# Weight splits held behind activation splits at two stage changes, the last FFN's gate and up projection turned round, and the last output columns cut 384 and 128

## The chip, the cores and the metric

One core of a Trainium2 chip runs the whole kernel. The metric is the time of one execution on the device in microseconds: the median of 3 runs of the kernel before is 1436.4 us (1436.33 to 1437.58). Engines by the profile's names: PE (TensorE, matrix products), PEld (its weight loads), DVE (VectorE), ACT (ScalarE), POOL (GpSimd), SP (SyncE, which issues nearly all DMAs).

## What is computed

Two transformer blocks over 256 tokens of width 1024, in float32:

```python
x = x + 0.5 * swiglu(rmsnorm(x), ...)           # FFN 1 (width 2816)
x = x + hybrid_mixer(rmsnorm(x), ...)           # mixer 1
x = x + 0.5 * swiglu(rmsnorm(x), ...)           # FFN 2
x = rmsnorm(x, final_norm)
h = ffn_sublayer(x + pos, ...); hc = ffn_sublayer(ctx, ...)   # FFN 3, 256 + 256 tokens
h = h + mods[5] * mixer(h, hc)                  # mixer 2
h = h + 0.5 * gate * ((silu(hn @ Wg) * (hn @ Wu)) @ Wd)       # FFN 4 ("the last FFN"), 256 tokens
return rmsnorm_2(h, g_final)
```

Shifts, scales and gates of the second block come from a small product with `w_ada`, which runs as a filler beside the other work.

## The kernel before

Every product is made of three: a float32 operand is split into a high and a low part (high by an ACT copy, low by a DVE subtraction), and high x high, high x low and low x high are accumulated (`mm3`, line 129, and `mm3r`, line 134, for several outputs in turn). A weight unit is 128 x 1024: `load` (line 96) fetches it by SP into one of 4 `raw` buffers, and `split` (line 107) writes `wh` (ACT) and `wl` (DVE), usually into one of 5 buffers each of the pool `wsp`, or into two of 18 slots (`salloc`, line 53). Activations are transposed on PE (line 147), and `split_out` (line 150) writes them as `XH` and `XL` (ACT, then DVE).

The order on each engine is fixed when the program is built. A scheduler goes by the order in which the code is written, but it issues ahead of its turn what it expects to be ready sooner. `tc.issue_after(ins)` keeps what is traced in its block behind `ins` on the same engine: an order of issue and no wait for `ins` to finish. Line 1110 uses it for one early unit.

**FFN 1, 2 and 4** (`ffn2tok`, line 316) take two token tiles of 128 tokens (t = 2 and 3). The up half runs over 11 chunks of 512 columns (256 of gate, 256 of up). In a chunk (`proj_chunk`, line 246) the activations are the stationary operand and the weights move, 512 columns at a time: 2 token tiles x 8 slices of K x 3 = 48 matmuls. `sink_gu` (line 331) makes silu(gate) * up with tokens on the partitions, and because the down half needs that transposed, `later` (line 343) adds 4 transposes to each chunk (line 348) and one `split_out`; they are issued in the next chunk (`flush_at=2`), those of the last chunk in the down half. In the down half each f of 22 brings one unit and 12 matmuls on 4 PSUM outputs of 512 (line 385). The last 4 f come output by output. With `fine` (last FFN) the last output of the last tile is made in two halves of 256 columns (line 396), so that the final norm can begin on the first. PSUM has 4 buffers of the tag `acc` and 4 of `tr`.

**FFN 3** (`ffn4tok`, line 413) has 512 tokens and does it the other way: weights stationary, tokens moving (`projT2`, line 303), so that the product comes out transposed. Its first 4 units (f = 0 and 1), split early into slots by `ahead` (line 1185), are used in halves of 256 tokens, which gives the second half of the tokens time to arrive.

**A change of stage** goes: last product, residual, norm (DVE, ACT, a power on POOL, DVE), 4 transposes for each half of a tile, XH, XL, first product of the next stage. `norm_end` (line 216) puts the transposes behind a number of matmuls of 512 columns that are traced after it: `late`, one number for each half (lines 1181, 1216, 1230). `self.last` (line 165) holds the two instructions of the newest `split_out` of a transposed half.

**Mixer 2** (`mixer2`, line 793) ends with the output projection `w_o` in two chunks (line 1064), the second tile by tile (`last_by_tile`), so that all its 4 units are split before its first tile is done. The last FFN's first chunk goes tile by tile too (`first_by_tile`).

The last function `after` (line 1238) makes the final norm of a tile and stores it in two DMAs of 512 columns (lines 1250 and 1252), one from ACT's queue and one from SP's.

## Time and profile before

| | us |
|---|---|
| median of 3 runs | 1436.4 |
| profiled execution, its own time | 1433.65 |
| span of the profiled execution, first to last instruction | 1431.8 |
| PE busy | 1408.0 |
| DVE busy | 920.8 |
| ACT busy | 627.2 |
| POOL busy | 32.6 |

The profile is of one execution. A row of the timeline gives the start in us from the span's beginning, the duration (of the merged group where a count follows), the engine, the line, the operation and what it writes and reads, how many were merged, and in brackets how long the engine stood idle before it and whose end let it go on. Matmuls are pipelined: one that shows 0.40 us can be followed 0.23 us later by the next, so the pace is read from the starts. Names of buffers in a row are not in the order of operands: `acc<-wh,XH` is a product of the two, whichever moves.

### The profile page before, as it was taken

What the parts mean: (1) busy time and instruction counts of PE and PEld (TensorE: products, weight loads), DVE (VectorE), ACT (ScalarE), POOL (GpSimd) and SP (SyncE); (2) the same over time, 40 slices, a digit from 0 to 9 for tenths busy, and PEclk for the clock granted to TensorE, in tenths of its full rate; (3) what the DMA queues carried; (4) which work ended last, traced back from release to release, by engine and by line L of the source; (5) the groups of instructions that cost most, each with busy time, mean ns of one, the idle gap of its engine ahead of it and who ended that gap; (6) DMA issues with size and microseconds to landing.
All of it is one profiled execution on the core that took longest, in us unless ns stands there. A gap on an engine that the chain in (4) does not pass through costs nothing. (4 is left out here: it accounts for less than half of the span.)

```text
span 1431.8 us, 17904 instructions
## 1 busy us (share of the span) xinstructions
PE 1408.0 (98%) x6782; PEld 1148.9 (80%) x6782; DVE 920.8 (64%) x1296; ACT 627.2 (44%) x904; POOL 32.6 (2%) x49
## 2 busy tenths in 40 slices
PE   7999999999999999999999999999999999999997
PEld 5877887778888888888888887889888888788886
DVE  6988456878988474543555447376886566755545
ACT  5445347465446442322122224353855454544442
POOL 0000000000000000000000001001010000000000
PEclk9999999999999999999999999999999999999999
DMA  8888645457887663643665443324236665555661
GB/s 285 297 267 271 213 135 196 133 178 251 301 276 244 211 213 105 193 146 102 191 205 176 152 142 103 108 101 143 87 120 189 192 192 177 183 182 180 184 183 71
DMA packets 73015, 260.65 MB, mean 182 GB/s; under 512 B 8140, under 2 KB 8672, under 8 KB 72928
## 3 DMA queue, kind: packets, MB, share of 16 engines
q1 hardware_dynamic: 72640, 258.98, 57.0%
q8 instruction: 53, 0.87, 0.2%
q10 hardware_dynamic: 288, 0.52, 0.1%
q14 instruction: 34, 0.28, 0.1%
HBM read 258.32 MB, written 1.14 MB: 181 GB/s over the span
## 5 line engine op out<-in xcount | busy, mean ns | idle before, releaser
L68 DVE TENSOR_TENSOR wl<-raw,wh 128x1024 fp32r<-128x1024 f32 (+1 forms) x385 | 464.3, 1211 | 335.7 <-ACT wh L65 331.6
L65 ACT ACTIVATE wh<-raw 128x1024 fp32r<-128x1024 f32 (+1 forms) x385 | 403.2, 1050 | 604.9 <-PE acc L78 466.5
L78 PE MATMUL acc<-wh,XH 128*128 128x512 f32 (+1 forms) x992 | 337.5, 398 | 0.3 <-ACT t L65 0.3
L78 PE MATMUL acc<-wh,XL 128*128 128x512 f32 (+1 forms) x992 | 333.7, 393 | 0.2 <-DVE XL L68 0.2
L78 PE MATMUL acc<-wl,XH 128*128 128x512 f32 (+1 forms) x992 | 332.0, 393 | 0.3 <-DVE wl L68 0.3
L78 PE MATMUL acc<-wh,S 128*128 128x512 f32 x872 | 237.3, 395 | 0.6 <-DVE t L71 0.6
L78 PEld LDWEIGHTS acc<-wh,XL 128*128 128x128 f32 x992 | 185.2, 188 | 42.6 <-DVE XL L68 1.3
L78 PEld LDWEIGHTS acc<-wl,XH 128*128 128x128 f32 x992 | 184.9, 188 | 42.4 <-DVE wl L68 1.8
L78 PEld LDWEIGHTS acc<-wh,XH 128*128 128x128 f32 x992 | 184.7, 188 | 41.4 <-ACT XH L65 0.5
L78 PEld LDWEIGHTS acc<-wh,S 128*128 128x128 f32 x872 | 162.8, 188 | 39.4 <-DVE t L71 1.4
L518 DVE SCALAR_TENSOR_TENSOR S<-raw,S 128x1024 f32<-128x1024 f32 x112 | 136.6, 1220 | 73.7 <-DMA raw<-in_w_ada 72.9
L78 PE MATMUL acc<-XH,wh 128*128 128x512 f32 (+1 forms) x456 | 137.3, 379 | 0.0
L78 PE MATMUL acc<-XL,wh 128*128 128x512 f32 (+1 forms) x456 | 137.2, 379 | 0.0
L78 PE MATMUL acc<-XH,wl 128*128 128x512 f32 (+1 forms) x456 | 137.2, 379 | 0.0
L78 PE MATMUL acc<-wl,S 128*128 128x512 f32 x436 | 132.6, 393 | 0.0
L78 PEld LDWEIGHTS acc<-XL,wh 128*128 128x128 f32 x456 | 83.9, 188 | 17.5
L78 PEld LDWEIGHTS acc<-XH,wl 128*128 128x128 f32 x456 | 83.9, 188 | 17.5
L78 PEld LDWEIGHTS acc<-XH,wh 128*128 128x128 f32 x456 | 83.7, 188 | 17.5
L78 PEld LDWEIGHTS acc<-wl,S 128*128 128x128 f32 x436 | 81.9, 188 | 18.5
L147 PE MATMUL tr<-ident,t 128*128 128x128 f32 x200 | 32.2, 285 | 11.6 <-DVE t L68 9.3
L65 ACT ACTIVATE XH<-tr 128x512 fp32r<-128x512 f32 x44 | 26.0, 597 | 37.9 <-PE tr L147 37.3
L78 PE MATMUL tr<-S,S 128*128 128x258 f32 (+3 forms) x288 | 42.0, 299 | 0.2 <-ACT S L65 0.2
(161 smaller groups left out, 855.9 us busy)
## 6 DMA issues: line engine op xcount, KB each, us to landing
raw<-in_gu SPq DMA_DIRECT2D x176, 512.0 KB, 4.3
raw<-in_d SPq DMA_DIRECT2D x88, 512.0 KB, 4.3
raw<-in_w_ada SPq DMA_DIRECT2D x72, 512.0 KB, 4.5
raw<-in_w_in SPq DMA_DIRECT2D x68, 512.0 KB, 3.8
raw<-in_w_qk SPq DMA_DIRECT2D x16, 512.0 KB, 3.6
bc<-modd SPq DMA_DIRECT2D x10, 512.0 KB, 4.9
raw<-in_w_out SPq DMA_DIRECT2D x8, 512.0 KB, 3.7
raw<-in_w_b SPq DMA_DIRECT2D x8, 512.0 KB, 4.2
```

Of the source, the lines that this page charges most:

```text
L65: return self.nc.scalar.activation(out=out, in_=in_, func=func, **kw)
L68: return self.nc.vector.tensor_tensor(out=out, in0=a, in1=b, op=op)
L78: self.nc.tensor.matmul(out, l, r, start=start, stop=stop, **kw)
L147: self.nc.tensor.transpose(tr[:, j, :], src[:, j * P:(j + 1) * P], self.ident)
L518: nc.vector.scalar_tensor_tensor(out=junk, in0=raw, scalar=1.0, in1=cb[r], op0=ALU.mult, op1=ALU.mult, accum_out=mc[:, o:o + 1])
```

## The change

Seven edits in one. First, `split` can hold its two instructions behind `self.last` on their engines while a counter `held` is above zero. Second, `ffn4tok` sets `held` to 4 after its first part, so the units of f = 2 and 3 are held. Third, mixer 2 calls `ahead` before the second `w_o` chunk: the last FFN's first 4 units are loaded and split there into 8 slots; after the last FFN's first chunk they are freed and `held` is 3. Fourth, in the last FFN the chunks 1 to 10 become 20 steps of `projT2` with stationary weights and 256 tokens moving, and the weights are packed to suit (`pack_guT`); silu * up then comes out transposed and is split directly. Fifth, at f = 0 of every down half of `ffn2tok` the matmuls of the first two outputs come before those of the other two. Sixth, `late` becomes (24, 27) at mixer 2 and (20, 23) at the last FFN. Seventh, the last output is made in 384 and 128 columns, and the final scaling of the first 128 columns goes from ACT to DVE, with a DMA of its own from SP.

```diff
@@ -35,6 +35,7 @@
         self.pre = []
         self.deferred = []
         self.later_pe = []
+        self.held = 0
 
 
     def nm(self, s):
@@ -110,8 +111,12 @@
         else:
             wh = self.wsp.tile([P, 1024], F32R, tag="wh", name=self.nm("wh"))
             wl = self.wsp.tile([P, 1024], F32R, tag="wl", name=self.nm("wl"))
-        self.act(wh[:, :n], raw[:, :n])
-        self.tt(wl[:, :n], raw[:, :n], wh[:, :n].bitcast(F32), ALU.subtract)
+        if self.held:
+            self.held -= 1
+            with self.tc.issue_after(self.last[0].ins), self.tc.issue_after(self.last[1].ins):
+                self.split_out(wh[:, :n], wl[:, :n], raw[:, :n])
+        else:
+            self.split_out(wh[:, :n], wl[:, :n], raw[:, :n])
         if self.fill_every:
             self.fill_count += 1
             if self.fill_count % self.fill_every == 0 and next(self.filler, 0) is None:
@@ -313,7 +318,7 @@
                 self.mm(ps, wl[:, s], a, False, k == xk - 1)
 
 
-    def ffn2tok(self, Wgu, Wd, xts, rows, sink, after, skew=4, first_by_tile=False, fine=False, mid=None, ahead=None):
+    def ffn2tok(self, Wgu, Wd, xts, rows, sink, after, skew=4, cols=False, first_by_tile=False, w0=(), fine=False, mid=None, ahead=None):
 
 
         hT = {}
@@ -324,7 +329,7 @@
                 hT[g] = (self.salloc([P, 4, 256], F32R), self.salloc([P, 4, 256], F32R))
             return hT[g] + (f % 4,)
 
-        for c in range(11):
+        for c in range(1 if cols else 11):
             self.fill_every = 2 if self.filler is not None and 1 <= c < 10 else 0
             trs = []
 
@@ -353,6 +358,24 @@
                 self.defer(later)
 
             self.proj_chunk(Wgu, 4 * c, xts, sink_gu, flush_at=2, last_by_tile=c == 0 and first_by_tile)
+            if c == 0 and w0:
+                for w in w0:
+                    self.sfree(*w)
+                self.held = 3
+        if cols:
+            toks = slice(xts[0][0] * P, xts[0][0] * P + 256)
+            for f in range(2, NF):
+                self.fill_every = 3 if self.filler is not None and f < 20 else 0
+                ws = [self.unit(Wgu[2 * f + j]) for j in range(2)]
+                pss = [self.psum("acc", [P, 256]) for _ in range(2)]
+                self.projT2(pss, ws, toks)
+                sil, h = self.t2([P, 256]), self.t2([P, 256])
+                self.act(sil, pss[0], AF.Silu)
+                self.tt(h, pss[1], sil, ALU.mult)
+                hh, hl, sl = dest(f)
+                self.split_out(hh[:, sl, :], hl[:, sl, :], h)
+                if f == 2:
+                    self.flush()
         if mid is not None:
             mid()
         ps = {}
@@ -382,7 +405,8 @@
                 self.mm3r(groups[3:], False, True)
                 sink(t, d, ps[t, d])
                 continue
-            self.mm3r(groups, f == 0, False)
+            for q in (groups[:2], groups[2:]) if f == 0 else (groups,):
+                self.mm3r(q, f == 0, False)
             if f == 0:
                 self.flush()
         ws = [self.unit(Wd[f]) for f in range(NF - skew, NF)]
@@ -393,8 +417,8 @@
         for i, (t, _) in enumerate(xts):
             for d in range(2):
                 if fine and i == 1 and d == 1:
-                    for q in (slice(0, 256), slice(256, 512)):
-                        pq = self.psum("tr", [P, 256])
+                    for q in (slice(0, 384), slice(384, 512)):
+                        pq = self.psum("tr", [P, q.stop - q.start])
                         for f in range(NF - skew, NF):
                             (wh, wl), (hh, hl, sl) = ws[f - NF + skew], dest(f)
                             w = slice(512 + q.start, 512 + q.stop)
@@ -441,6 +465,7 @@
                 for w in ws:
                     self.sfree(*w)
                 f = 2
+                self.held = 4
             for f in range(f, f1):
                 self.fill_every = 1 if f0 + 4 < f or f0 else 0
                 ws = [self.unit(Wgu[2 * f + j]) for j in range(2)]
@@ -790,7 +815,7 @@
         self.stt(out, z, 0.0, e, ALU.min, ALU.subtract)
 
 
-    def mixer2(self, xts, x, after):
+    def mixer2(self, xts, x, after, ahead):
         nc, A = self.nc, self.A
         lat = xts[2:]
         W = A["w_in2"]
@@ -1061,6 +1086,8 @@
                 self.tt(x[t][:, s], x[t][:, s], y, ALU.add)
                 after(t, n)
 
+            if n == 1:
+                ahead()
             self.proj_chunk(A["w_o"], 4 * n, [(t, mx[t]) for t, _ in lat], sink_o, last_by_tile=n == 1)
         self.sfree(*H.values(), *MX.values(), *SO.values(), *GA.values())
 
@@ -1213,7 +1240,7 @@
         def after(t):
             if t == 0:
                 prep()
-            xm.append((t, self.norm_xT(x[t], t, *mods[1 if t < 2 else 0], (21, 24))))
+            xm.append((t, self.norm_xT(x[t], t, *mods[1 if t < 2 else 0], (24, 27))))
 
         self.ffn4tok(A["gu3"], A["d3"], xts, res_gate, after, w3)
         self.sfree(x[0], x[1], *mods[0], *mods[1])
@@ -1227,9 +1254,17 @@
                 mods[2] = (self.mod_scale(7, 0, gF), self.mod(6, 0))
             fin[t] = self.norm_half(x[t], fin.get(t), d, mods[2][0])
             if d == 1:
-                xf.append((t, self.norm_end(fin[t], t, mods[2][1], (18, 21))))
-
-        self.mixer2(xm, x, after)
+                xf.append((t, self.norm_end(fin[t], t, mods[2][1], (20, 23))))
+
+        w4 = []
+
+        def ahead():
+            for u in range(4):
+                dst = self.salloc([P, D], F32R), self.salloc([P, D], F32R)
+                w4.append(self.split(*self.load(A["gu4"][u]), dst))
+
+        self.mixer2(xm, x, after, ahead)
+        self.pre = list(w4)
         G[0] = self.mod(8, 0)
         gl = self.bcast(A["g_final"])
 
@@ -1246,12 +1281,15 @@
             if d == 0 or q.stop < 512:
                 return
             r = self.rstd_of(ss, len(part))
-            self.act(ys[0], ys[0], scale=r)
-            nc.scalar.dma_start(out=self.out[t - 2][:, 0:512], in_=ys[0])
+            o = self.out[t - 2]
+            self.act(ys[0][:, 128:], ys[0][:, 128:], scale=r)
+            nc.scalar.dma_start(out=o[:, 128:512], in_=ys[0][:, 128:])
             self.ts(ys[1], ys[1], r)
-            nc.sync.dma_start(out=self.out[t - 2][:, 512:], in_=ys[1])
-
-        self.ffn2tok(A["gu4"], A["d4"], xf, {}, res_gate, after, first_by_tile=True, fine=True)
+            nc.sync.dma_start(out=o[:, 512:], in_=ys[1])
+            self.ts(ys[0][:, :128], ys[0][:, :128], r)
+            nc.sync.dma_start(out=o[:, :128], in_=ys[0][:, :128])
+
+        self.ffn2tok(A["gu4"], A["d4"], xf, {}, res_gate, after, first_by_tile=True, fine=True, w0=w4, cols=True)
 
 
 COLS = [("b_a", 2), ("conv_w", 12), ("gnorm", 1), ("wa2", 256), ("qk_w", 48), ("qk_b", 16),
@@ -1303,6 +1341,12 @@
     return pack_proj(w)
 
 
+def pack_guT(g, u):
+
+    gt, ut = pack_T(g), pack_T(u)
+    return np.concatenate([pack_gu(g, u)[:4], np.stack([gt, ut], axis=1)[2:].reshape(-1, P, D)])
+
+
 def pack_d4(w):
     parts = []
     for f0, f1 in ((0, 12), (12, 22)):
@@ -1341,7 +1385,7 @@
     a["gu1"] = pack_gu(i["ffn1_w_gate"][0], i["ffn1_w_up"][0])
     a["gu2"] = pack_gu(i["ffn2_w_gate"][0], i["ffn2_w_up"][0])
     a["gu3"] = pack_T(i["w_ffn1_in_2"][0]).reshape(2, NF, P, D).transpose(1, 0, 2, 3).reshape(2 * NF, P, D)
-    a["gu4"] = pack_gu(i["w_ffn2_in_2"][0][:, :FF], i["w_ffn2_in_2"][0][:, FF:])
+    a["gu4"] = pack_guT(i["w_ffn2_in_2"][0][:, :FF], i["w_ffn2_in_2"][0][:, FF:])
     a["d1"] = i["ffn1_w_down"][0].reshape(NF, P, D)
     a["d2"] = i["ffn2_w_down"][0].reshape(NF, P, D)
     a["d3"] = pack_d4(i["w_ffn1_out_2"][0])
```

## Rows read from the trace of the kernel before

**Rows 1.** The page: engine totals, bandwidth in 40 slices, one group of weight loads.
```profile
PE 1408.0 (98%) x6782; PEld 1148.9 (80%) x6782; DVE 920.8 (64%) x1296; ACT 627.2 (44%) x904; POOL 32.6 (2%) x49
...
GB/s 285 297 267 271 213 135 196 133 178 251 301 276 244 211 213 105 193 146 102 191 205 176 152 142 103 108 101 143 87 120 189 192 192 177 183 182 180 184 183 71
...
L78 PEld LDWEIGHTS acc<-wh,XH 128*128 128x128 f32 x992 | 184.7, 188 | 41.4 <-ACT XH L65 0.5
```

**Rows 2.** Waits of PE: who waited for whom; us in total, times, longest.
```profile
PE tr L147 <- DVE t L71: 2.2, 3, 1.1
PE acc L78 <- DVE XL L68: 2.0, 2, 1.8
```

**Rows 3.** Timeline of PE where FFN 1's down half begins.
```profile
143.69 1.68 PE L78 MATMUL acc<-wh,S 128*128 128x512 f32 x6 [0.62 <-DVE t L71]
```

**Rows 4.** Timelines of PE, DVE, ACT, POOL at the change from FFN 2 to FFN 3.
```profile
510.82 0.40 PE L78 MATMUL acc<-XH,S 128*128 128x256 f32 x2
...
522.83 0.63 PE L147 MATMUL tr<-ident,t 128*128 128x128 f32 x4 [0.62 <-DVE t L71]
...
526.87 0.51 PE L78 MATMUL acc<-XL,S 128*128 128x256 f32 x2 [1.77 <-DVE XL L68]
527.21 0.63 PE L78 MATMUL acc<-XH,S 128*128 128x256 f32 x4
...
538.04 0.62 PE L78 MATMUL acc<-XH,wh 128*128 128x512 f32 x2
...
523.87 2.35 DVE L68 TENSOR_TENSOR wl<-raw,wh 128x1024 fp32r<-128x1024 f32 x2
526.14 1.28 DVE L68 TENSOR_TENSOR XL<-tr,XH 128x512 fp32r<-128x512 f32 x2
...
524.42 0.60 ACT L65 ACTIVATE XH<-tr 128x512 fp32r<-128x512 f32 x1 [0.32 <-PE tr L147]
...
511.92 1.37 POOL L197 TENSOR_TENSOR sm<-sm,mhalf 128x1 f32<-128x1 f32 x1 [3.48 <-ACT sm L65]
```

**Rows 5.** Timelines of DVE and POOL at the very end.
```profile
1423.48 0.42 DVE L68 TENSOR_TENSOR t<-tr,bc 128x256 f32<-128x256 f32 x1
...
1426.68 0.55 POOL L197 TENSOR_TENSOR sm<-sm,mhalf 128x1 f32<-128x1 f32 x1 [5.69 <-issue]
```

**Rows 6.** Timelines of PE, DVE, ACT, POOL from `w_o` to the last FFN.
```profile
1224.34 0.39 PE L78 MATMUL acc<-wh,XH 128*128 128x512 f32 x1
...
1231.21 1.29 PE L147 MATMUL tr<-ident,t 128*128 128x128 f32 x8 [1.13 <-DVE t L71]
...
1245.24 0.63 PE L78 MATMUL acc<-wh,XH 128*128 128x512 f32 x2
...
1230.31 1.41 DVE L71 SCALAR_TENSOR_TENSOR t<-t,sm,bc 128x512 f32<-128x512 f32 x2 [0.44 <-POOL sm L197]
...
1225.98 1.06 ACT L65 ACTIVATE wh<-raw 128x1024 fp32r<-128x1024 f32 x1 [2.82 <-issue]
...
1227.56 1.04 ACT L65 ACTIVATE wh<-raw 128x1024 fp32r<-128x1024 f32 x1
...
1228.87 1.41 POOL L197 TENSOR_TENSOR sm<-sm,mhalf 128x1 f32<-128x1 f32 x1 [135.00 <-ACT sm L65]
```

**Rows 7.** Timeline of PE at the change from FFN 3 to mixer 2.
```profile
885.49 0.63 PE L147 MATMUL tr<-ident,t 128*128 128x128 f32 x4 [0.43 <-DVE t L71]
```

**Rows 8.** Chunks 1 to 10: busy PE, PEld, DVE, ACT, POOL; clock, DMA, GB/s. Timeline, one flush.
```profile
1245.25:1361.51 116.26, 116.26 (x521) 94.03 (x520) 63.59 (x71) 53.83 (x70) 0.00 (x0) 1.00 0.61 190
...
1265.27 0.60 PE L348 MATMUL tr<-ident,t 128*128 128x128 f32 x4
...
1265.94 0.39 PE L78 MATMUL acc<-wl,XH 128*128 128x512 f32 x1
```

**Rows 9.** Timeline of PE in mixer 2's Q projection, 256 columns moving.
```profile
986.10 0.40 PE L78 MATMUL acc<-XH,wh 128*128 128x256 f32 x2
...
991.80 0.40 PE L78 MATMUL acc<-XH,wh 128*128 128x256 f32 x2
```

## The prediction

> **What bounds the kernel now.** First the engine totals: PE is busy for 1408.0 of 1431.8 us, DVE for 920.8, ACT for 627.2 [rows 1]. So only three things can shorten the time: work taken from PE, a wait of PE that goes, or the two ends where PE has nothing to do. Next the waits of PE, sorted by total [rows 2]. They are few. Leaving out the start of the kernel, which the change doesn't touch, transposes waited 2.2 us on the last step of a norm (L71), in three places, and products waited 2.0 us for XL. Then the timeline of PE at each of these places, and beside it DVE, ACT and POOL: there one sees what stood in front of the instruction that was waited for. Last the pace of PE, which has to be read from starts, since a matmul shows more time than it takes from the next.
>
> The profiled execution took 1433.65 us, 2.75 less than the median of 1436.4 us. The sum is made against the former, and the same difference is taken from the latter. A measurement of this kernel can tell about 0.2%, 2.9 us, from no change.
>
> **Order at f = 0 (fifth edit).** In FFN 1's down half the third matmul waits 0.62 us for DVE to empty the PSUM buffer of the last chunk [rows 3]. Two matmuls of free buffers stand ahead of it now, six after the change. Four more at 0.233 us (the pace derived below) are 0.93 us, more than the wait. Gain 0.6, bounds 0 and 0.6. FFN 2 and 4 show no such wait now; what the last FFN gets is priced below.
>
> **FFN 2 to FFN 3 (first and second edit).** From 510.82 to 538.04 PE makes 4 x 48 = 192 matmuls of 256 columns and 4 groups of transposes. The last 92 of them, from 527.21 to 538.04, run at 0.1177 us each; 192 are 22.6. A group of transposes costs 0.44 (below), four 1.8. That is 24.4 of 27.2 us: 2.8 us are lost here. Two waits are named: 1.77 us for XL, 0.62 us for the norm [rows 4]. The first is plain: XH of the second half is done at 525.02, and XL could follow, but DVE makes two weight splits first (523.87, 2.35 us), so the two XL start at 526.14. These splits belong to f = 2 and 3, which start at 538.04. Behind XL they cost 4 x 1.18 us of DVE and less on ACT, over by about 531: nothing waits. Their `raw` buffers stay full some 2 to 5 us longer, so SP's queue, where the filler's loads stand too, pauses for as long; FFN 3's next units are needed only after f = 3. The second wait is the last step of a chain through POOL: its power took 1.37 us at 511.92 [rows 4] with a weight split on DVE, and 0.55 at the end of the kernel, where none runs [rows 5]. With the splits gone the chain should come 0.8 us sooner, more than the wait. I take 1.8 + 0.6 = 2.4; bounds 1.7 (the norm stays late) and 2.8.
>
> **`w_o` to the last FFN (third edit, and part of the sixth).** From 1224.34 to 1245.24 PE makes 24 + 48 matmuls of 512 and 4 groups of transposes: 72 x 0.233 + 1.8 = 18.5 of 20.9 us, so 2.4 are lost, 1.13 of them in one wait for the norm [rows 6]. In that chain POOL's power takes 1.41 us, again beside weight splits, and the norm's step starts at 1230.31, when w_o's last matmul has already been issued. After the change these four units are split before, and the next three are held. The chain then is 0.86 us shorter on POOL (0.55 for 1.41), and two weight copies of 1.06 and 1.04 us no longer stand in it on ACT [rows 6]: up to 3.0 us in all. The 20 matmuls ahead of the first transposes end at 1224.34 + 20 x 0.233 = 1229.0, so 1.3 us are enough. I expect no wait there, and 2.2 us back. Against that stand four extra splits in the stretch before: 4 x 1.18 us of DVE, 2.1 MB of DMA. The loads run at 177 to 184 GB/s there and at up to 301 elsewhere [rows 1]; 2.1 MB more over the 22 us of w_o ask for about 275. The slots are old ones, free for long. If one of these splits gets in front of an XL that `w_o` waits for, it costs up to 1.2 us; I take 0.2. Net gain 2.0; bounds 1.0 and 2.4.
>
> **Entry of mixer 2 (rest of the sixth).** The wait here is 0.43 us [rows 7]. By the starts, 27 of the last tile's 30 matmuls go ahead of these transposes, where the scheduler moved them, not the 21 asked for. Asking for 24 moves nothing. Gain 0; bounds 0 and 0.4.
>
> **The last FFN's up half (fourth edit).** Before, ten chunks take 116.26 us, 11.63 each [rows 8]. The four transposes of a flush cost the way from 1265.27 to 1265.94 less one matmul, 0.67 - 0.23 = 0.44. So a matmul of 512 takes (11.63 - 0.44) / 48 = 0.233. After, a chunk is 96 matmuls of 256 with the weights stationary, the same columns, and no transposes (one group remains, that of chunk 0). The nearest row is mixer 2's Q projection: the same helper, the same pool of weights, the same 256 tokens. There 48 matmuls take 991.80 - 986.10 = 5.70 us [rows 9], so a chunk takes 11.40. Gain 10 x 0.23 = 2.3. The far end is FFN 3's first part at 0.1177: 11.30, gain 3.3 [rows 4]. Below, without the pace, is the turnover rival. DVE and ACT, 63.6 and 53.8 us in 116.3, get two splits of 256 for one of 512 per chunk: 0.42 us for 256 columns [rows 5] against 0.70 for 512 (half of 1.41, [rows 6]), 0.14 more for each. They have room.
>
> On weight loads: 480 are added, each shown with 0.188 us [rows 1], but two matmuls with their loads take 0.2375 us together [rows 9], so loads run beside matmuls. The Trainium skill, page "TensorE: Matmul & The Clock Gate", section "The mechanism", says that a weight load overlaps running matmuls only when it uses other rows of the array; all of these use all rows. By that rule the edit would lose far more than it gains; rows 9 speak against it here.
>
> At the end of that half the down half needs the PSUM buffers of f = 21, whose silu and product both end after the last matmul. Six matmuls of free buffers, 1.4 us, cover them. A weight split in front of them adds up to 1.2. I take a loss of 0.2; bounds 0 and 1.0.
>
> **The tail (seventh edit).** DVE sets it: after the last matmul it still works through the halves of 256 at 0.42 us each step [rows 5]. By 0.42 for 256 and 0.70 for 512, a step on 384 takes about 0.56 and one on 128 about 0.28 (estimates from these two). The sum of a step over both pieces stays; the last piece is 0.14 shorter in its residual and in its square; but the tile before gets an extra scaling on DVE, ahead of all that, and the last tile a third DMA. PE pays for 12 matmuls of 128 somewhere between half and all of a 256: up to 0.7 us more, behind which DVE still has older work. Net 0; bounds -0.4 and +0.4.
>
> **Sum.** 0.6 + 2.4 + 2.0 + 0 + 2.3 - 0.2 + 0 = 7.1 us, 1426.6 for the profiled execution, 1429.3 for the median. With all bounds together: 9.9 gained (1426.5), or 3.0 (1433.4).
>
> **Rivals.**
> - *The hold does less than it says* (20%): it is an order of issue only, and the scheduler rearranges around it; another long instruction takes the place of the split. Half of 2.4 + 2.0 is lost: 1431.5.
> - *A wait takes the place of the one removed* (11%): the held splits, the extra ones before `w_o`, or the change to the down half cost PE 1.2 us each, and Q's pace isn't reached: 7.1 - 3 x 1.2 - 1 = 2.5, 1433.9.
> - *More* (8%): FFN 3's pace and the entry of mixer 2 as well: 7.1 + 1.0 + 0.4 = 8.5, 1427.9, and with the bounds of the others 1426.5.
> - *Weight buffers turn over too late* (5%, slower): a step of the up half uses two of five buffers for its whole 5.70 us and frees both at its end. If the second split of the next but one step comes one DVE split (1.18 us) late, 20 steps lose 23.6: 1452.9. It decides from 7.1 / 20 = 0.36 us a step on. For it speaks that before, a buffer came free every 2.8 us; against it, that Q runs with just this turnover at 5.70 [rows 9].
> - *Loads are not hidden* (1%): 480 x 0.188 = 90 us, about 1522. The section of the Trainium skill named above would have it so; rows 9 refute it.
>
> **How the numbers follow.** The forecast has 55%, and its own range is 1427 to 1432. With "does less" and "more" 83% lie below 1433.5 (faster by over 0.2%); the replaced wait, 11%, lies within 0.2%; 5 + 1% are slower. The range from 1426.0 to 1434.0 takes in all bounds and most of the replaced wait.
>
> **What would show it.** In the profile after: no wait for XL near 525, and four weight splits behind the XL there; the transposes after `w_o` in two groups, without a wait over 0.3; PE at 0.119 a matmul in the last FFN's up half, without L348 in it; the third matmul of FFN 1's down half without its wait. Wrong would be: PE waiting for a weight split in the up half, for XL in the first `w_o` chunk, or for a sink at the start of the last down half.

## The result and the profile after

The changed kernel takes 1426.89 us (median of 5 runs, 1426.11 to 1428.03) beside 1436.4 us of the kernel before, measured in turn with it (1435.08 to 1437.58). The ratio is 0.9934, with a 95% interval of 0.992 to 0.9949: faster, by 9.5 us. The profiled execution took 1426.11 us, 7.5 less than the profiled one of before. The forecast was 1429.3 us, with a range of 1426.0 to 1434.0.

The page of the changed kernel, engine totals (busy us, share of the span, instructions; the span is 1424.3 us); they answer to the first row of [rows 1].

```profile
PE 1404.2 (99%) x7222; PEld 1170.0 (82%) x7222; DVE 919.5 (65%) x1308; ACT 626.5 (44%) x914; POOL 29.3 (2%) x49
```

PE has 440 matmuls and loads more (480 for 256 columns, less 40 transposes), and is busy 3.8 us less. The rest of the gain is waits. The waits of PE in the changed kernel (who waited for whom; us in total, times, longest), which answer to [rows 2]:

```profile
PE tr L152 <- DVE t L72: 0.8, 3, 0.4
PE acc L79 <- DVE t L72: 0.4, 1, 0.4
...
PE acc L79 <- DVE XL L69: 0.2, 1, 0.2
```

The 1.8 us wait for XL is gone and so is the 1.1 us wait of the transposes: of the 4.2 us of [rows 2] 1.0 is left. (The second row here is the wait at f = 0, 0.62 us in [rows 3].) Where the span went can be summed by stretches of PE, each from the start of one named matmul to that of the next. The columns are the stretch, its length, then busy time of PE, PEld, DVE, ACT and POOL, the granted clock, the DMA share and GB/s. First the kernel before: `w_o` from its first matmul to the first one of its last tile in the second chunk (72 of its 96 matmuls), from there to the last FFN, its chunk 0, its last down half, the end.

```profile
1206.67:1224.34 17.67, 17.67 (x81) 14.27 (x80) 12.96 (x17) 7.84 (x11) 0.00 (x0) 1.00 0.59 172
1224.34:1232.52 8.18, 6.99 (x33) 5.17 (x31) 6.56 (x9) 5.45 (x8) 1.41 (x1) 1.00 0.31 94
1232.52:1245.24 12.72, 12.59 (x56) 9.76 (x57) 10.50 (x15) 7.56 (x11) 0.98 (x1) 1.00 0.52 164
...
1361.51:1420.38 58.87, 58.87 (x257) 47.64 (x256) 28.76 (x29) 21.72 (x25) 0.00 (x0) 1.00 0.44 133
1420.38:1431.85 11.47, 2.98 (x25) 2.77 (x23) 5.36 (x12) 3.49 (x9) 1.10 (x2) 0.83 0.24 92
```

The same stretches of the changed kernel, with FFN 3's first part ahead and chunks 1 to 10 of the last FFN (the fifth row):

```profile
510.64:535.14 24.50, 24.50 (x210) 24.49 (x209) 17.91 (x26) 11.78 (x22) 1.65 (x3) 1.00 0.62 209
...
1203.54:1221.62 18.08, 17.89 (x82) 14.07 (x80) 15.20 (x19) 8.74 (x12) 0.00 (x0) 1.00 0.73 251
1221.62:1228.08 6.46, 6.46 (x33) 5.29 (x32) 4.08 (x7) 1.65 (x5) 0.55 (x1) 1.00 0.00 0
1228.08:1240.26 12.18, 12.18 (x57) 9.71 (x56) 8.28 (x13) 7.75 (x12) 0.55 (x1) 1.00 0.14 47
1240.26:1354.61 114.35, 114.35 (x965) 114.35 (x964) 62.02 (x82) 53.62 (x81) 0.00 (x0) 1.00 0.63 194
1354.61:1412.64 58.03, 58.03 (x254) 47.17 (x253) 29.55 (x30) 22.38 (x26) 0.00 (x0) 1.00 0.46 144
1412.64:1424.30 11.66, 3.56 (x25) 3.41 (x23) 5.89 (x14) 3.27 (x9) 1.10 (x2) 0.77 0.25 91
```

| stretch | before | after | difference | forecast |
|---|---|---|---|---|
| start to the end of FFN 1's down half | 206.29 | 205.99 | -0.3 | -0.6 |
| FFN 3, first part [rows 4] | 27.22 | 24.50 | -2.7 | -2.4 |
| `w_o`, first 72 of 96 matmuls | 17.67 | 18.08 | +0.4 | +0.2 |
| from there to chunk 1 of the last FFN | 20.90 | 18.64 | -2.3 | -2.2 |
| chunks 1 to 10 [rows 8] | 116.27 | 114.35 | -1.9 | -2.3 |
| last down half | 58.87 | 58.03 | -0.8 | +0.2 |
| from its fine pieces to the end | 11.47 | 11.66 | +0.2 | 0 |
| all the rest | | | -0.1 | 0 |
| span | 1431.8 | 1424.3 | -7.5 | -7.1 |

The start scatters: in the fourteen profiled executions of this study FFN 1's down half began between 141.4 and 145.3 us, since FFN 1 waits for its weights to arrive (the DMA moves 269 to 307 GB/s in the first four slices of the page). Two medians are therefore compared with about 2 us of doubt, while a stretch behind that point that a run leaves alone repeats mostly within some hundredths of a microsecond (FFN 3's first part took 24.48 to 24.50 us in the kernels that keep the hold and all addresses); `w_o` with the early loads doesn't (run 3). The experiments are read from stretches first.

### The profile page after: what moved, and what is told of

Its sections match the earlier page's. It is cut to its first block, busy times and chain, and to the rows that moved or that the text cites. A ratio compares the mean times of both kernels' runs of the same rounds, so it can differ in the third digit from the quotient of the medians.

```text
span 1424.3 us, 18795 instructions
## 1 busy us (share of the span) xinstructions
PE 1404.2 (99%) x7222; PEld 1170.0 (82%) x7222; DVE 919.5 (65%) x1308; ACT 626.5 (44%) x914; POOL 29.3 (2%) x49
## 5 line engine op out<-in xcount | busy, mean ns | idle before, releaser
L79 PE MATMUL acc<-wh,XH 128*128 128x512 f32 (+2 forms) x816 | 277.3, 398 | 0.4 <-ACT t L66 0.4
L79 PE MATMUL acc<-wh,XL 128*128 128x512 f32 (+2 forms) x816 | 273.4, 393 | 0.2 <-DVE XL L69 0.2
L79 PE MATMUL acc<-wl,XH 128*128 128x512 f32 (+2 forms) x816 | 272.4, 392 | 0.0
L79 PE MATMUL acc<-XH,wh 128*128 128x512 f32 (+1 forms) x776 | 201.5, 339 | 0.0
L79 PE MATMUL acc<-XH,wl 128*128 128x512 f32 (+1 forms) x776 | 201.2, 339 | 0.0
L79 PE MATMUL acc<-XL,wh 128*128 128x512 f32 (+1 forms) x776 | 201.1, 339 | 0.0
L79 PEld LDWEIGHTS acc<-wh,XL 128*128 128x128 f32 x816 | 152.2, 189 | 34.6 <-DVE XL L69 1.1
L79 PEld LDWEIGHTS acc<-XL,wh 128*128 128x128 f32 x776 | 133.0, 188 | 17.5
L79 PEld LDWEIGHTS acc<-XH,wl 128*128 128x128 f32 x776 | 132.9, 188 | 17.5
L79 PEld LDWEIGHTS acc<-XH,wh 128*128 128x128 f32 x776 | 132.9, 188 | 17.5
```

Of the source, the lines that this page charges most:

```text
L79: self.nc.tensor.matmul(out, l, r, start=start, stop=stop, **kw)
```

## The experiments

All of them start from the changed kernel. Each was timed in turn with the kernel before, 4 to 11 runs of each.

**1. Without the hold at FFN 3 (e1_free_ffn3).**
```diff
-                self.held = 4
```


> The changed kernel without the hold at FFN 3 (second edit undone, all else kept). Theory (the hold puts two weight splits behind XL, and takes splits off DVE while POOL computes the norm's power): the 192 matmuls of FFN 3's first part take 27.2 us again instead of 24.5, PE waits about 1.8 us for XL and 0.6 for the norm, POOL's powers there take 1.0 to 1.4 us again instead of 0.55; 2.7 us slower than the changed kernel. Rival (only the place of the two splits before XL counts, POOL is not part of it): 1.8 slower, powers stay at 0.55. Rival (the gain is a reshuffled order that would come with any edit): under 0.5 slower.

Measured: 1432.1 us, ratio 0.9972 (0.9963 to 0.9981). FFN 3's first part takes 28.05 us instead of 24.50. Timelines of this kernel (start, duration, engine, line, operation; in brackets the idle time before and what ended it), PE, DVE and POOL at the change from FFN 2 to FFN 3:

```profile
526.02 0.63 PE L152 MATMUL tr<-ident,t 128*128 128x128 f32 x4 [1.46 <-DVE t L72]
530.06 0.50 PE L79 MATMUL acc<-XL,S 128*128 128x256 f32 x2 [1.80 <-DVE XL L69]
...
527.05 2.35 DVE L69 TENSOR_TENSOR wl<-raw,wh 128x1024 fp32r<-128x1024 f32 x2
529.32 1.28 DVE L69 TENSOR_TENSOR XL<-tr,XH 128x512 fp32r<-128x512 f32 x2
...
515.11 1.37 POOL L202 TENSOR_TENSOR sm<-sm,mhalf 128x1 f32<-128x1 f32 x1 [3.48 <-ACT sm L66]
```

And of the changed kernel, where the hold stands:

```profile
523.14 0.69 DVE L69 TENSOR_TENSOR XL<-tr,XH 128x512 fp32r<-128x512 f32 x1 [1.37 <-ACT XH L66]
524.05 0.69 DVE L69 TENSOR_TENSOR XL<-tr,XH 128x512 fp32r<-128x512 f32 x1 [0.22 <-ACT XH L66]
525.00 4.63 DVE L69 TENSOR_TENSOR wl<-raw,wh 128x1024 fp32r<-128x1024 f32 x4 [0.25 <-ACT wh L66]
...
515.42 0.55 POOL L202 TENSOR_TENSOR sm<-sm,mhalf 128x1 f32<-128x1 f32 x1 [3.86 <-ACT sm L66]
```

Both waits come back with the two splits ahead of XL, and with them the slow power on POOL. With the hold, the four splits stand behind the last XL in one block, and the four powers of this stretch take 0.55 us each. The hold is worth 3.6 us in this pair and 2.7 in that of before and after, so neither rival stands: the loss is over 1.8 us, and the power is slow again.

**2. The early loads without the hold behind chunk 0 (e7_ahead_no_hold).**
```diff
-                self.held = 3
```


> The changed kernel without the hold behind the last FFN's first chunk (held = 3 left out), the early loads and splits of gu4 kept. It parts the 2.26 us gained at the start of the last FFN. Theory A, the early splits alone bring it (the engines have nothing to split while tile 3's norm is due): c0 to c1 and the stretch ahead of it stay at 6.46 and 12.18 us, the time within 0.3 us of 1426.9. Theory B, the hold is needed as at FFN3: the next weight splits run ahead of tile 3's splits, 1 to 2 us come back, 1428 to 1429 us.

Measured: 1429.35 us, ratio 0.9963 (0.9949 to 0.9976). The stretches are 18.52, 8.18 and 12.59 us. PE, DVE and POOL of this kernel behind `w_o`:

```profile
1229.00 1.29 PE L152 MATMUL tr<-ident,t 128*128 128x128 f32 x8 [1.10 <-DVE t L72]
...
1224.88 1.23 DVE L69 TENSOR_TENSOR wl<-raw,wh 128x1024 fp32r<-128x1024 f32 x1 [0.40 <-ACT wh L66]
1226.44 1.23 DVE L69 TENSOR_TENSOR wl<-raw,wh 128x1024 fp32r<-128x1024 f32 x1 [0.33 <-ACT wh L66]
...
1226.67 1.41 POOL L202 TENSOR_TENSOR sm<-sm,mhalf 128x1 f32<-128x1 f32 x1 [135.62 <-ACT sm L66]
```

And the changed kernel there:

```profile
1226.29 0.60 PE L152 MATMUL tr<-ident,t 128*128 128x128 f32 x4
...
1227.41 0.60 PE L152 MATMUL tr<-ident,t 128*128 128x128 f32 x4
...
1225.04 1.41 DVE L72 SCALAR_TENSOR_TENSOR t<-t,sm,bc 128x512 f32<-128x512 f32 x2 [1.01 <-POOL sm L202]
...
1224.46 0.55 POOL L202 TENSOR_TENSOR sm<-sm,mhalf 128x1 f32<-128x1 f32 x1 [133.50 <-ACT sm L66]
```

Theory B: without the hold the early loads gain nothing. The three stretches take 39.29 us together, 36.72 in the changed kernel and 38.57 in the one before. (What a hold would bring without the early loads, no run shows.) Without the hold the next weights' splits fill the time that the early ones left free, POOL's power takes 1.41 us again and the transposes wait 1.10 us, as before the change.

**3. Neither early loads nor that hold (e3_no_ahead).** The call of `ahead` in mixer 2, `self.pre = list(w4)` and `w0=w4` are left out, and `late` is (18, 21) again at the last FFN.


> The changed kernel without the early loads and splits of the last FFN's first 4 units and without the hold of the next 3 (third edit undone), late back to 18 and 21 there. Theory (weight splits stood in the chain from w_o's sink to the transposes, on ACT, on DVE and beside POOL's power): from the second w_o tile's first matmul to the second chunk or step of the last FFN 20.9 us again instead of 18.6, one wait of about 1.1 us for the norm, the power at 1.4 us; against it 0.4 us come back before, at the first w_o chunk, where the early splits stand in front of DVE work that PE waits for. Net 1.8 us slower than the changed kernel. Rival (only the order behind the last XL counts, as at FFN 3): about 0.3 slower, since no XL was waited for here.

Measured: 1430.16 us, ratio 0.9959 (0.9946 to 0.9972). The same three stretches and the last down half:

```profile
1202.82:1220.51 17.69, 17.69 (x81) 14.26 (x80) 12.97 (x17) 7.84 (x11) 0.00 (x0) 1.00 0.54 172
1220.51:1228.69 8.18, 7.00 (x34) 5.17 (x32) 6.56 (x9) 5.45 (x8) 1.40 (x1) 1.00 0.35 101
1228.69:1241.40 12.71, 12.59 (x57) 9.77 (x57) 10.50 (x15) 7.56 (x11) 0.98 (x1) 1.00 0.58 161
1355.74:1414.30 58.56, 58.56 (x254) 47.18 (x253) 29.55 (x30) 22.39 (x26) 0.00 (x0) 1.00 0.47 143
```

All of before's times are back, 1.86 us more over the three stretches than in the changed kernel, as expected. `w_o`'s 17.7 us are back too: the early splits cost 0.4 us there. In the eleven executions that have them at this place, `w_o` took 18.05 to 19.30 us, 18.5 on average, so 0.8 is their usual price. And the last down half is 0.53 us longer, though nothing of it was touched. That is taken up below (runs 8 to 12).

**4. The early loads one stage earlier (e6_ahead_early).**
```diff
+            if n == 1:
+                ahead()
             self.proj_chunk(W, 32 + 4 * n, lat, lambda t, ps: self.act(GA[t][:, s], ps, AF.Sigmoid))
...
-            if n == 1:
-                ahead()
             self.proj_chunk(A["w_o"], 4 * n, [(t, mx[t]) for t, _ in lat], sink_o, last_by_tile=n == 1)
```


> The changed kernel with the four early loads and splits of gu4 (ahead) called before the second GA projection chunk instead of before the second w_o chunk. Theory A, these splits take ScalarE and VectorE from the mixer's own splits behind w_a and so cost the w_o stretch time: from the first to the second w_o chunk's tile 17.7 us as in the kernel before instead of 18.1 to 19.3, 0.4 to 1.6 us less, 1425.5 to 1426.7 us; the GA chunk's sinks run on ScalarE alone and have slack. Theory B, the spread of that stretch has another cause (when the raw loads land): it stays at 18.1 or above and the time at 1427 us.

Measured: 1428.58 us, ratio 0.9952 (0.9938 to 0.9965). `w_o`'s stretch is 17.69 us, as theory A has it: the splits were the cause. But the time is not lower. From mixer 2's Q projection to `w_a` it takes 200.52 us instead of 199.30, with a new wait in it that the changed kernel doesn't have:

```profile
1163.48 0.63 PE L152 MATMUL tr<-ident,t 128*128 128x128 f32 x4 [0.99 <-DVE t L69]
```

DVE of this kernel just before, an early split (into a slot, `S`) ahead of the products that the transposes wait for:

```profile
1160.91 1.23 DVE L69 TENSOR_TENSOR S<-raw,S 128x1024 fp32r<-128x1024 f32 x1 [1.04 <-ACT S L66]
...
1162.65 1.28 DVE L69 TENSOR_TENSOR t<-S,S 128x512 f32<-128x512 f32 x2
```

The splits stand in front of another stage's steps there and cost 1.2 us, more than the 0.4 that `w_o` got back. (Another 3.0 us of this execution were lost in the start, which the edit doesn't touch.)

**5. The old form of the last up half (e2_old_up).** `cols=True` and `pack_guT` are left out.


> The changed kernel with the last FFN's up half as before: activations stationary, 512 weight columns moving, transposes (fourth edit undone, its packing too; first units early and hold kept). Theory (40 transposes cost 0.44 per four, matmuls of 256 cost 0.1187 against 0.233 for 512): chunks 1 to 10 take 116.3 instead of 114.35, and the down half 0.4 more for the last transposes; 2.3 to 2.8 us slower than the changed kernel. Rival (the gain in the down half, 0.8 us, has to do with the up half only by chance): 1.9 slower, with the down half as in the changed kernel.

Measured: 1428.94 us, ratio 0.9962 (0.9948 to 0.9976). Chunks 1 to 10 and the last down half:

```profile
1240.23:1356.14 115.91, 115.91 (x521) 94.35 (x520) 64.81 (x73) 54.32 (x71) 0.00 (x0) 1.00 0.64 195
1356.14:1414.44 58.30, 58.30 (x257) 47.69 (x256) 28.77 (x29) 21.59 (x25) 0.00 (x0) 1.00 0.45 135
```

The new form is worth 115.91 - 114.35 = 1.56 us in the up half and 0.27 in the down half, whose transposes for the last chunk it removes. The other 0.36 us by which 115.91 lies under 116.27 is the pace of the old form's matmuls, which is not the same in the two kernels (about 1 ns a matmul; why, no run shows). Up and down half together lose 1.83 us, less than the 2.3 to 2.8 expected.

**6. The old order at f = 0 (e4_old_f0).**
```diff
-            for q in (groups[:2], groups[2:]) if f == 0 else (groups,):
-                self.mm3r(q, f == 0, False)
+            self.mm3r(groups, f == 0, False)
```


> The changed kernel with the old order at f = 0 of the down halves (fifth edit undone). Theory after seeing the changed trace (the wait has only moved back by four matmuls, since the same product waits for DVE's h, which waits for a weight split that came late from DMA): no difference, FFN 1's down half from first matmul to the flush's end within 0.1 us of 4.0. Rival (the forecast): 0.6 us slower. Rival for the last FFN: without the edit its third matmul waits for f = 21's product, up to 1 us slower.

Measured: 1428.92 us, ratio 0.9953 (0.9941 to 0.9965). Where FFN 1's down half begins, this kernel, then the changed one:

```profile
144.33 1.65 PE L79 MATMUL acc<-wh,S 128*128 128x512 f32 x6 [1.28 <-DVE t L72]
```
```profile
144.22 1.35 PE L79 MATMUL acc<-wh,S 128*128 128x512 f32 x4 [0.45 <-DVE t L72]
```

The wait doesn't go, it moves from the third matmul to the seventh. Its size differs from run to run: 0.62 us [rows 3] and 1.28 us in the old order; none to 0.81 us, 0.35 on average, in the twelve kernels with the new one. The averages differ by 0.6 us, but there are only two executions of the old order, and 4.0 us from the first matmul to the end of the flush, which the theory gave for this kernel, were 4.68. The rival for the last FFN falls: no wait comes there, and its down half takes 58.20 us beside 58.03. (1.2 us of this execution's time went into `w_o`, 19.30 us, by the early splits of run 3.)

**7. The old end (e8_old_tail).** Pieces of 256 and 256, the first half of the output scaled and stored at once.


> The changed kernel with the old end: last columns 256 and 256, the first half of the output scaled and stored in one piece. The forecast put the tail at 0 with bounds of 0.4 either way; the traces had 11.46 us before and 11.68 after from the fine pieces' first matmul to the end. Theory A, the new end costs what the traces show: 11.4 to 11.5 us here, 0.2 us less than the changed kernel. Theory B, the difference is the scatter of the last store's landing: 11.6 to 11.8 us, no difference.

Measured: 1427.04 us, ratio 0.9945 (0.9933 to 0.9958). From the fine pieces to the end:

```profile
1413.57:1425.14 11.57, 3.00 (x25) 2.79 (x23) 5.36 (x12) 3.48 (x9) 1.10 (x2) 0.80 0.24 92
```

That lies between 11.47 and 11.66. In the twelve executions with the new end this stretch took 11.44 to 11.75 us, 11.66 on average; the two with the old end took 11.47 and 11.57. So the new end gains nothing and costs about 0.1 us, if anything; DVE's busy time in it grows from 5.36 to 5.89 us, which is the added scaling (0.68 us twice where 0.49 stood).

**8. XH, XL and the slots at other places (e5_xh_xl_moved).** This and the next four runs go after the 0.5 us of the last down half. By each matmul's time to the start of the next, grouped by the buffers of its operands, hT's slots had different paces: in before, slots 8 to 12 as stationary operand 233.3 ns, slots 4 to 7 and 13 to 17 about 228 to 230. (Modulo 512 bytes of a partition, XH and XL begin at 160, slots 4 to 7 at 224, 8 to 12 at 256, 13 to 17 and the weight buffers `wh` and `wl` at 288.) `ahead` takes eight slots, so that hT of the last FFN (two slots for each group of four f, high and low part) moves from (1,12), (3,11), (2,8), (4,7), (5,13), (14,6) to (5,13), (14,6), (15,10), (17,9), (16,0), (1,12): 231.7 ns before, 229.7 after.
```diff
+            tc.tile_pool(name="slots_a", bufs=1) as slots_a, \
+            tc.tile_pool(name="xhp", bufs=1) as xhp, \
+            tc.tile_pool(name="slots_b", bufs=1) as slots_b, \
+            tc.tile_pool(name="xlp", bufs=1) as xlp, \
+            tc.tile_pool(name="slots_c", bufs=1) as slots_c, \
```


> The changed kernel with one thing altered: where its buffers lie in SBUF. XH takes the place that slots 4 to 7 had, XL that of slots 13 to 16, the slots move around them; every instruction and its order stay as they are. In the traces of before and after, 512-column matmuls whose stationary operand lies in slots 4 to 7 or 13 to 17 start 227 to 230 ns apart, those in slots 8 to 12 233.3 ns, those in XH and XL 232.8 ns (2400 of them). Theory A, the pace follows the place in SBUF of the stationary operand: the 2400 matmuls on XH and XL go to 228 to 230 ns, 2400 x 3 to 4.5 ns = 7 to 11 us less, with some us either way for the down halves, whose slots move too: 1416 to 1421 us beside 1426.9 for the changed kernel. Theory B, the pace goes with what the matmuls compute, or with what the other engines do in that stretch, and the agreement with the slots is chance: XH and XL stay at 232.8 ns, 1426 to 1428 us.

Measured: 1426.46 us, ratio 0.9939 (0.9926 to 0.9951). XH 232.8 ns as before, XL 231.3 instead of 232.8, and every slot kept its pace, though slots 0 to 11 now lie 32768 bytes lower and 12 to 16 16384 lower. Theory A as put falls: it isn't the place as such. Theory B doesn't hold either, XL changed. What stayed for the slots is their offset within a round number of bytes.

**9. All slots at odd multiples of 32 bytes (e9_slots_32).**
```diff
+        for i in range(NSLOT):
+            self.slots.tile([P, 1040], F32, tag=f"S{i}", name=f"S{i}_0")
...
+        padp.tile([P, 8], F32, tag="pad", name="pad")
```


> The changed kernel with only addresses altered: the slots stand 4160 bytes apart in a partition instead of 4096 or 4128, and start 32 bytes later, so that each begins at an odd multiple of 32 bytes (32 modulo 64). In e5_xh_xl_moved the slots moved by whole multiples of 16384 bytes and each kept its pace, and the matmuls whose stationary hT began at a multiple of 64 took 233 ns, those at an odd multiple of 32 took 227 to 230. Theory A, the pace of hT's matmuls follows that offset: all four down halves run at 228 to 229 ns, about 264 x 2.7 + 264 x 2.7 + 520 x 2 + 250 x 0.7 ns = 2.6 us less than the changed kernel, 1424 to 1425 us. Theory B, the full distance to the moving weights counts (only two of the offsets tried were fast, 224 and 288 modulo 512): some slots fast, some slow, no net change, 1426 to 1427.5 us.

Measured: 1429.7 us, ratio 0.9953 (0.994 to 0.9965). hT's matmuls take 231.5 ns on average over the four down halves instead of 230.7, single slots 227 to 235. Theory A falls.

**10. XH and XL at the weights' offset (e10_xh_slots_32).** As run 9, and
```diff
+        self.cpool.tile([P, 32], F32, tag="padx", name="padx")
         self.XH = self.cpool.tile([P, 8, 512], F32R, tag="XH", name="XH")
...
+        padw.tile([P, 96], F32, tag="padw", name="padw")
```


> As e9_slots_32, and XH and XL begin 128 bytes later (at 288 modulo 512 instead of 160, the offset of the weight buffers and of slots 13 to 17); the weight buffers keep their offset modulo 512. Theory A, XH and XL at 288 behave as hT does there: their 2400 512-column matmuls go from 232.8 to between 228.5 and 231.2 ns (the value that XL had at 288 in e5_xh_xl_moved), 4 to 10 us less beside e9_slots_32, and the 2352 with XH and XL moving may gain as well: 1414 to 1421 us. Theory B, streams in which each matmul has another stationary operand keep 232.8 ns whatever the offset: as e9_slots_32.

Measured: 1416.2 us, ratio 0.9861 (0.9846 to 0.9877). The matmuls with XH or XL stationary take 227.9 ns, those with XH or XL moving 226.8 instead of 232.8. hT stays at 231.8, though its slots lie 128 bytes further too. (`padw` keeps the weight buffers at 288.) Theory A: 13.5 us less than run 9, from 128 bytes.

**11. The weight buffers 32 bytes later (e11_wsp_32).**
```diff
+        padw.tile([P, 8], F32, tag="padw", name="padw")
```


> The changed kernel with only the weight buffers wh and wl 32 bytes later (0 modulo 64 instead of 32); slots, XH and XL stay. Theory A, it is the offset of the stationary operand itself that counts: each slot keeps its pace, the last down half stays at 229.0 ns. Theory B, stationary and moving operand have to agree modulo 64: the paces of the slots change places, slots 8 to 12 (multiples of 64) go to 228 to 230 and slots 4 to 7 and 13 to 17 to 233, the last down half to 233 ns, 250 x 4 ns = 1 us more there, and XH and XL change as well, by up to 4 ns x 2400 either way.

Measured: 1434.43 us, ratio 0.9988 (0.9979 to 0.9997): nearly all that the change had gained is lost by 32 bytes. XH and XL go to 234.1 ns, hT to 232.2. Slots 4 to 7 and 13 to 17 are now slow (mostly 232 to 234 ns), slots 8 to 11 fast in FFN 1 and 3 (226 to 231), but in FFN 2 they stay at 233.3 ns. So it is the relation of the two operands' addresses, but an agreement modulo 64 alone doesn't say which is fast.

**12. All of them at one offset (e12_all_288).** XH, XL, the slots, `wh` and `wl` at 288 modulo 512 bytes.
```diff
+        for i in (0, 1, 3, 7, 12):
+            self.slots.tile([P, 1152], F32, tag=f"S{i}", name=f"S{i}_0")
...
+        padp.tile([P, 8], F32, tag="pad", name="pad")
...
+        self.cpool.tile([P, 32], F32, tag="padx", name="padx")
```


> The changed kernel with only addresses altered: XH and XL begin 128 bytes later as in e10_xh_slots_32, the slots keep 4096 bytes each (4608 for five of them), and XH, XL, all 18 slots, wh and wl begin at 288 modulo 512 bytes of a partition. In e10_xh_slots_32 the streams whose operands both began at 288 took 226.5 to 228 ns a matmul, in e9, e10 and e11 hT's streams took 228 to 236 ns with the slots at mixed offsets. Theory A, operands that begin at the same offset modulo 512 run fast, whichever they are: XH and XL at 227.5 as in e10, and hT, whose slots now all agree with the weights, at 228 ns in all four down halves instead of e10's 232.3, 231.1, 231.9 and 231.5: 264 x 4.3 + 264 x 3 + 520 x 3.9 + 250 x 3.5 ns = 4.8 us less than e10_xh_slots_32, 1410 to 1413 us. Theory B, only XH and XL matter by their place and hT's pace has another cause: down halves at 231 to 232 ns, 1415 to 1417 us.

Measured: 1411.81 us (1410.06 to 1412.3), ratio 0.9831 (0.9817 to 0.9844): 24.5 us less than the kernel before and 15.1 less than the changed one, without one instruction altered. Two stretches, FFN 3's up half from f = 2 to 11 (480 matmuls on XH and XL) and the last down half; first the changed kernel, then e10, e11 and e12. (The second row of the changed kernel stands above.)

```profile
535.14:646.79 111.65, 111.65 (x484) 90.45 (x483) 54.91 (x75) 29.99 (x40) 0.00 (x0) 1.00 0.48 152
```
```profile
533.63:642.63 109.00, 109.00 (x483) 90.15 (x482) 55.11 (x75) 29.96 (x40) 0.00 (x0) 1.00 0.51 156
1344.43:1402.92 58.49, 58.49 (x254) 47.24 (x253) 29.55 (x30) 22.37 (x26) 0.00 (x0) 1.00 0.47 144
```
```profile
538.10:650.20 112.10, 112.10 (x483) 90.12 (x482) 54.88 (x75) 30.03 (x40) 0.00 (x0) 1.00 0.49 151
1362.22:1420.97 58.75, 58.75 (x255) 47.14 (x253) 29.55 (x30) 22.40 (x26) 0.00 (x0) 1.00 0.46 143
```
```profile
532.68:641.63 108.95, 108.95 (x483) 90.14 (x482) 54.63 (x75) 29.95 (x40) 0.00 (x0) 1.00 0.50 156
1341.27:1398.63 57.36, 57.36 (x254) 47.17 (x253) 29.54 (x30) 22.33 (x26) 0.00 (x0) 1.00 0.48 147
```

The clock is granted in full in all of them, and PE is busy throughout, with no wait: only the pace differs. Theory A: hT takes 227.1 ns on average (single slots 226 to 229). It also shows that the 0.5 us of the last down half can be had, or lost, by the slots alone.

## Why the prediction was right, and where it was off

**The sum** was 7.1 us and the profiled pair shows 7.5; its time was forecast as 1426.6 and is 1426.1. That it came so close is partly luck: the last down half gave 1.0 us more than forecast, 0.5 of it by a term that no step had, and this makes up for f = 0, `w_o` and the last up half, which gave less. The lower bounds that the steps name add up to 3.6 us, not to the 3.0 of the sum. **The step from there to the median** was off by 2.0 us, more than the sum: the profile of before lay 2.75 us below its median, and that was carried over. The profile of after lies 0.8 below its own. It was a scatter of that one execution and not a constant of the kernel (perhaps of its start; no second profile of the kernel before shows it); 2.0 of the 2.4 us between forecast and result are this.

**FFN 2 to FFN 3.** Forecast 2.4 us, found 2.7, near the upper bound of 2.8. The powers of POOL went from 1.37 to 0.55 us as the step has it, and run 1 brings both back with the splits. The choice to leave 0.4 us of the loss unexplained was too careful: with the splits away, PE has no wait here at all (24.50 busy of 24.50). A second power there, 0.99 us beside the norm's multiplication in the kernel before (rows in the last section), became 0.55 us too, which the step had not counted.

**`w_o` to the last FFN.** 2.2 us back and 2.26 found, with POOL, the norm and the transposes as described. (The norm's step needed to come 2.0 us sooner, not 1.3, since its first piece of 0.70 us has to be done when the transposes start; it came 2.55 sooner, 3.42 us behind the stretch's beginning instead of 5.97.) The price of the early splits was sized too low, at 0.2: 0.4 in this pair and 0.8 on average. The mechanism was named, a split in front of something that `w_o` waits for, but it is the sinks of `w_a`, two steps on DVE for each tile, that stand behind it, not XL. DVE of the changed kernel at the start of `w_o`:

```profile
1201.57 1.23 DVE L69 TENSOR_TENSOR S<-raw,S 128x1024 fp32r<-128x1024 f32 x1 [0.58 <-ACT S L66]
...
1203.32 1.22 DVE L69 TENSOR_TENSOR wl<-raw,wh 128x1024 fp32r<-128x1024 f32 x1
1204.45 0.69 DVE L69 TENSOR_TENSOR t<-t,S 128x512 f32<-128x512 f32 x1
```

An early split (into a slot, `S`) lies ahead of the sink's first step and a regular one (`wl`) ahead of its second, where the kernel before has the two steps on end; the transposes behind them wait 0.19 us here and 1.47 us in run 6's execution. Run 4 moves the early splits and the loss goes with them, to another stage.

**The last up half.** Forecast 2.3 us, found 1.9, and 1.56 against the old form in the changed kernel's slots (run 5). The pace was right: 114.35 us less one group of transposes (0.36 by the starts around 1245.95) are 0.1187 us for each of 960 matmuls, against 5.70 / 48 = 0.1188 from [rows 9]. The step forgot in its sum the group of transposes that it had itself said remains. PEld is busy for all of the 114.35 us and costs nothing: the loads run beside the matmuls. The section "The mechanism" of the page "TensorE: Matmul & The Clock Gate" of the Trainium skill says that a load overlaps running matmuls only where it goes to other rows of the array; this trace doesn't agree with that, as [rows 9] had shown. The same section also has loads into a background weight buffer pulled ahead of running matmuls; the trace would fit that, but can't show it.

**The last down half** was to lose 0.2 us by a late sink. No such wait is there: DVE was done in time. Instead it gained 0.8. 0.3 of this are the transposes of the last chunk, which f = 0 had flushed there and which the forecast had not booked (runs 3 and 5: 58.87 - 58.56, 58.30 - 58.03). The other 0.5 are the pace of its matmuls, a term that no step had.

**f = 0.** Forecast 0.6; about 0.6 between averages, 0.17 in the pair's waits, and the reason was half wrong. Four more matmuls were to outlast the wait. It stays in nine of twelve kernels, up to 0.81 us long: the DVE step that empties the buffer comes later in some executions than in others. I take it that this follows when the weights land in this DMA-bound stage; no run tested that.

**Mixer 2 and the tail.** Both were put at 0 and gave 0 and +0.2, within their bounds; the tail's steps on DVE took 0.55 us on 384 columns and 0.29 on 128, as interpolated.

**The rivals.** "The hold does less" falls by runs 1 and 2, "buffers turn over too late" and "loads not hidden" by the up half's 114.35 us, "more" by its pace of 0.1187 us and the wait of 0.4 us that is left at mixer 2. Of "a wait takes the place" a part came true, 0.4 to 0.8 us in `w_o`. Of the signs of being wrong, none is in the profile; of the signs of being right, two are off in a detail: the third matmul's wait moved to the seventh, and the last up half still has the one group of transposes (L353 now) that the step had named.

## What to carry to other kernels

At a change of stage, look at what an in-order engine has queued ahead of the last step that PE waits for: work for later that is ready early is not free there, and a hold behind that step was worth 2 to 4 us at each of two places, on top of early loads, while early loads without it were worth nothing at the one place where that was run. Carry no difference between one profiled execution and its median from one kernel to the next. And where a kernel is bound by PE's pace, compare the pace of equal matmuls on different buffers before counting instructions: the addresses may hold more than the order.

## What the runs showed of the hardware

The pace of equal matmuls depends on where their operands lie in SBUF. Mean time from one 512-column matmul to the next, ns, at the full granted clock (without those followed by a wait or by transposes):

| kernel | XH, XL stationary (2400) | XH, XL moving (1176) | hT stationary (1308) | time, us |
|---|---|---|---|---|
| changed | 232.8 | 232.8 | 230.7 | 1426.89 |
| e5 | 232.3 | 232.2 | 230.6 | 1426.46 |
| e9 | 232.7 | 232.9 | 231.5 | 1429.7 |
| e10 | 227.9 | 226.8 | 231.8 | 1416.2 |
| e11 | 234.1 | 233.3 | 232.2 | 1434.43 |
| e12 | 227.7 | 226.7 | 227.1 | 1411.81 |

Where all operands began at the same offset modulo 512 bytes of a partition, the streams took 227 to 228 ns; elsewhere 226 to 235, by slot, and 230 or more on average. By these means e12 should save 2400 x 5.1 + 1176 x 6.1 + 1308 x 3.6 ns = 24 us; the span fell by 13.9. FFN 1 waits for its weights in any case (its down half began at 142.23 us and at 143.01; PE in e12 waits 1.7 us for weight splits there), so 2.7 us of its 528 matmuls are not gained and 0.8 are lost; the transposes in FFN 2 wait 1.4 us for DVE, and the 256-column matmuls of the last up half went the other way, from 114.35 to 115.63 us. That is about 6 of the 10 us that are missing. Where the rest went, why the 256-column matmuls are slower, which address bits count, and why slots 8 to 11 were slow in FFN 2 and fast in FFN 1 and 3 of run 11, stays open: no run parted these.

POOL's power on 128 x 1 took 0.55 us alone and 0.73 to 1.48 beside DVE instructions with two inputs in SBUF. The kernel before at 517.06 us, beside the norm's multiplication, then the changed kernel, beside an XL, one input of which (`tr`) lies in PSUM:

```profile
517.06 0.68 DVE L68 TENSOR_TENSOR t<-x,bc 128x512 f32<-128x512 f32 x1
517.16 0.99 POOL L197 TENSOR_TENSOR sm<-sm,mhalf 128x1 f32<-128x1 f32 x1 [3.86 <-ACT sm L65]
```
```profile
518.69 0.69 DVE L69 TENSOR_TENSOR XL<-tr,XH 128x512 fp32r<-128x512 f32 x1
519.17 0.55 POOL L202 TENSOR_TENSOR sm<-sm,mhalf 128x1 f32<-128x1 f32 x1 [3.21 <-ACT sm L66]
```

In the fourteen traces 80 of these powers began while DVE ran a weight split or a norm's multiplication, and each of them ended 0.40 to 0.42 us after that DVE instruction (here 517.06 + 0.68 + 0.41 = 518.15), so a power that begins just behind the start of a split loses the most. That was one of the two ways in which a split delayed a norm. The page "GPSIMD Engine Reference" of the Trainium skill, section "Specifications", lists POOL's SBUF interface as shared with VectorE, with contention beside VectorE instructions that have two SBUF inputs, as a weight split has. The traces agree with that, with the sizes above.
